# Hybrid trunk layer: order of the mixer's column pairs, four attention chains in step, and a fourth seven-product unit in the first branch gates

## Chip, cores and metric

The kernel runs on one core of one Trainium2 chip. The metric is the device time of one execution in microseconds, and the median of several runs is the kernel's time. Traces come from one further execution under the hardware profiler.

## The reference

One layer of a trunk on x (1, 256, 2048): a SwiGLU half-step, a mixer of two gated recurrences side by side, a second SwiGLU half-step, with an RMSNorm before and behind each. The change touches only the mixer:

```python
proj = u @ w_in
(g_q, g_k, g_v, g_out, g_code, h_q, h_f, h_i, h_out, z_gla, z_hgrn) = jnp.split(proj, offsets, axis=-1)
...
o_gla = merge_heads(rms_norm(o_gla, gla_norm)).astype(u.dtype) * jax.nn.silu(g_out)
...
log_f = jnp.logaddexp(jnp.log(lb), jnp.log1p(-lb) + jax.nn.log_sigmoid(h_f.astype(jnp.float32)))
h_k = -jnp.expm1(log_f)
o_hgrn = chunked_gated_linear_attention(
    split_heads(jax.nn.silu(h_q), HGRN_HEADS), split_heads(h_k, HGRN_HEADS),
    split_heads(h_i, HGRN_HEADS), split_heads(log_f, HGRN_HEADS))
...
merged = (jax.nn.sigmoid(z_gla + b_branch_gates[0]) * (o_gla @ w_branch_gla)
          + jax.nn.sigmoid(z_hgrn + b_branch_gates[1]) * (o_hgrn @ w_branch_hgrn))
return merged @ w_out
```

GLA has 4 heads (key width 128, value width 256), HGRN2 has 8 heads of 128. Both are causal recurrences with a decay for each key element.

## The kernel before

**Stages.** The layer runs as FFN1, mixer, FFN2. The 256 rows are two tiles of 128 (t = 0, 1). Weights come from HBM in float32, in chunks of two 128-row tiles by 512 columns. Each is split into a high part (`whi`, ScalarE's copy, L158) and a low part (`wlo`, VectorE's subtraction, L160). Every product is then three matmuls: high by high, high weight by low operand, low weight by high operand (L164, L165, L166). All operands are laid out beforehand, so TensorE waits for nothing but weights.

**Pairs.** The mixer's projections are computed in pairs of 512-wide column blocks (`gemm_pair`, called by `two`). The 2048 rows of the contraction make eight units of two row tiles. A plain unit is two chunks (one for each block), with 12 matmuls for each. Some units are seven-product units (`seven`): a Strassen-like scheme takes 7 products of three matmuls instead of 8, and pays with sums of weights (`wsum`, `raw`) that VectorE forms, ScalarE copies (`wsumh`) and VectorE splits (`wsuml`). The sums of the operand x for them are made once, by `operand_sums`. With the sums of three units (`SUMS`) a pair has three sevens; once a fourth unit's sums are there (`FOUR`), four. At the end of a pair `share` and `close` add the products that the sevens share (`psum`) to the accumulators c in PSUM. A ring of five buffers holds split weights, and three hold the rows of sums. `steps` is the order of chunks and sevens in a pair; with `late` the sevens stand at places 6, 8 and 10.

**Side work.** What isn't a projection is written as generators that `Side.pump` advances, once for each plain chunk and twice in a seven. Light ones are transposes, gates and dots: each yields and goes on one step at a pump. Heavy ones are the attention chains (`attention`), one for each row tile and branch group: seven levels (1, 2, 4, ... 64 wide), in each of which TensorE multiplies small blocks (L899, 32 matmuls in the trace for a narrow level), VectorE scales k and q (L915, L918), picks scores (`own`, L920) and multiplies decays into totals (`tot`, L939). `full` holds the heavy ones off around a seven; with `fast` they step at each pump where no light one is left, else at every second; at most two chains step in one pump. The instructions of all this stand in one order for each engine, which the program fixes when it is built: an engine issues strictly in that order, and a split behind a level waits for the level.

**The mixer's pairs** are, in order: GK/GV, GV+CB/GO, GO+CB/HF, HI/HO, HQ+CB/HF+CB, HI+CB/HO+CB, then the first two branch gates ZG (a pair), two branch blocks, and the other gates and blocks (G is GLA, H is HGRN; Q, K, V, O are queries, keys, values and output gates, F forget gates, I HGRN's values; +CB is the second block of 512 columns). The GLA chains (two row tiles) begin behind the first pair, the first HGRN chains behind the third, the second behind the fifth. The forget gates are computed by `hgrn_gates`: transposes, two sigmoids (L1068, L1069), and for each of four heads two affine copies with the lower bound, "borders" below (L1072, L1073).

## Time and profile before

| | |
|---|---|
| median of 3 runs | 2053.48 us (2053.33 to 2054.65) |
| the profiled execution | 2053.87 us |
| its span in the trace | 2052.0 us |
| granted TensorE clock, mean | 0.998 |
| HBM read and written | 406.11 MB, 4.19 MB |
| ScalarE | 1331.7 us busy, 65% |

A row of a timeline gives the start of an instruction (or of a run of like ones, "x2"), its length, engine and line, the tiles out<-in, and in brackets the idle time before it with what ended it. Instructions of one engine overlap at their ends, so that the distance from start to start is what an engine pays for one; where VectorE has an x2 row, the next row's start tells. PE is TensorE, DVE VectorE, ACT ScalarE.

### The profile page before, as it was taken

The page shows a single profiled execution, that of the slowest core. Times are in us where ns is not written, and L with a number is a line of the kernel's source. Part 1 is how long each engine was busy: PE and PEld are TensorE (multiplying, and loading weights), DVE is VectorE, ACT ScalarE, POOL GpSimd, SP SyncE. Part 2 cuts the span into 40 slices and gives each one's busy share as a digit, 9 for nine tenths or more (in the row PEclk, how much of TensorE's full clock was granted, in tenths as well). Part 3 has the DMA queues.
Part 4 walks back from the last instruction along what each step waited for, and adds up shares of the span by engine and source line. Part 5 has one row for each costly group of instructions (what it writes and reads, how often), then busy time and mean ns, then how long its engine had stood idle before and what let it go on. Part 6 is the DMA issues. An engine that isn't in the chain of part 4 may idle for free.

```text
span 2052.0 us, 29001 instructions
## 1 busy us (share of the span) xinstructions
PE 2039.7 (99%) x10287; PEld 1696.1 (83%) x10287; DVE 1896.4 (92%) x2237; ACT 1331.7 (65%) x1740; POOL 40.1 (2%) x87
## 2 busy tenths in 40 slices
PE   9999999999999999999999999999999999999998
PEld 8888888888888888878888888888888888888886
DVE  8999999999899889989999898889999999989997
ACT  7666666666666577577655565666666766676663
POOL 1000000000000100000000000010000000000000
PEclk9999999999999999999999999999999999999999
DMA  8777677776657567556566568757777777776664
GB/s 254 228 215 230 200 220 223 214 223 212 224 183 234 163 215 226 164 173 194 169 199 196 180 219 226 233 161 207 245 199 222 220 215 208 220 235 195 216 194 144
DMA packets 256282, 425.60 MB, mean 207 GB/s; under 512 B 72116, under 2 KB 80503, under 8 KB 256136
## 3 DMA queue, kind: packets, MB, share of 16 engines
q1 hardware_dynamic: 196624, 401.80, 62.0%
q10 hardware_dynamic: 59512, 21.94, 5.6%
q8 instruction: 80, 1.31, 0.3%
q14 instruction: 66, 0.54, 0.1%
HBM read 406.11 MB, written 4.19 MB: 200 GB/s over the span
## 4 chain that ended last, share of the span: by engine, by line
PE 92%; DVE 3%; ACT 2%; DMA 2%; issue 1%; POOL 0%; SPq 0%; DVEq 0%; POOLq 0%; ACTq 0%
PE c L164 22%; PE c L165 22%; PE c L166 22%; PE p L166 6%; PE p L164 6%; PE p L165 6%; PE mm L164 2%; PE mm L166 2%; PE mm L165 2%; DVE h L546 1%; PE ps L404 1%; DVE wlo L160 1%; DVE held L160 1%; DMA raw<-in_w_in_dram 1%; PE ps L899 0%
## 5 line engine op out<-in xcount | busy, mean ns | idle before, releaser
L158 ACT ACTIVATE whi<-raw 128x1024 fp32r<-128x1024 f32 (+3 forms) x486 | 491.6, 1025 | 176.7 <-PE c L165 75.7
L160 DVE TENSOR_TENSOR wlo<-raw,whi 128x1024 fp32r<-128x1024 f32 (+3 forms) x486 | 567.9, 1182 | 38.4 <-ACT whi L158 36.1
L164 PE MATMUL c<-whi,xhi 128*128 128x512 f32 (+1 forms) x1350 | 526.1, 390 | 0.7 <-DVE hq L842 0.5
L165 PE MATMUL c<-whi,xlo 128*128 128x512 f32 (+1 forms) x1350 | 522.7, 387 | 0.0
L166 PE MATMUL c<-wlo,xhi 128*128 128x512 f32 (+1 forms) x1350 | 522.2, 387 | 0.0
L250 DVE TENSOR_TENSOR wlo<-raw,whi 128x1024 fp32r<-128x1024 f32 x264 | 313.9, 1218 | 17.6 <-ACT whi L289 14.3
L164 PEld LDWEIGHTS c<-whi,xhi 128*128 128x128 f32 x1350 | 253.4, 188 | 52.2 <-issue 1.2
L166 PEld LDWEIGHTS c<-wlo,xhi 128*128 128x128 f32 x1350 | 253.4, 188 | 50.7 <-DVE wlo L160 0.2
L165 PEld LDWEIGHTS c<-whi,xlo 128*128 128x128 f32 x1350 | 253.5, 188 | 49.2
L289 ACT ACTIVATE whi<-raw 128x1024 fp32r<-128x1024 f32 x132 | 139.6, 1057 | 214.1 <-DVE raw L250 141.7
L250 DVE TENSOR_TENSOR wsuml<-wsum,wsumh 128x1536 fp32r<-128x1536 f32 x132 | 231.1, 1751 | 12.7 <-ACT wsumh L291 12.7
L164 PE MATMUL c<-whi,hkhi 128*128 128x512 f32 x534 | 207.7, 389 | 0.0
L165 PE MATMUL c<-whi,hklo 128*128 128x512 f32 x534 | 207.7, 389 | 0.0
L166 PE MATMUL c<-wlo,hkhi 128*128 128x512 f32 x534 | 207.7, 389 | 0.0
L287 ACT ACTIVATE wsumh<-wsum 128x1024 fp32r<-128x1024 f32 x132 | 138.8, 1051 | 87.4 <-DVE wsum L250 42.9
L285 ACT ACTIVATE whi<-raw 128x1024 fp32r<-128x1024 f32 x132 | 139.1, 1054 | 73.5 <-PE c L165 49.3
L250 DVE TENSOR_TENSOR wsum<-raw,raw 128x1024 f32<-128x1024 f32 x132 | 160.9, 1219 | 22.8 <-DMA raw<-in_ffn_w_down_dram 13.2
L165 PEld LDWEIGHTS c<-whi,hklo 128*128 128x128 f32 x534 | 100.2, 188 | 20.9
L164 PEld LDWEIGHTS c<-whi,hkhi 128*128 128x128 f32 x534 | 100.2, 188 | 20.9
L166 PEld LDWEIGHTS c<-wlo,hkhi 128*128 128x128 f32 x534 | 100.2, 188 | 20.7
L250 DVE TENSOR_TENSOR c<-c,psum 128x512 f32<-128x512 f32 x143 | 94.4, 690 | 8.7 <-PE c L166 8.4
L250 DVE TENSOR_TENSOR wsum<-raw 128x512 f32<-128x512 f32 x132 | 91.2, 691 | 3.8
(347 smaller groups left out, 3072.0 us busy)
## 6 DMA issues: line engine op xcount, KB each, us to landing
raw<-in_ffn_w_down_dram SPq DMA_DIRECT2D x120, 512.0 KB, 4.8
raw<-in_w_in_dram SPq DMA_DIRECT2D x104, 512.0 KB, 4.4
raw<-in_ffn_w_gate_dram SPq DMA_DIRECT2D x90, 512.0 KB, 4.6
raw<-in_ffn_w_up_dram SPq DMA_DIRECT2D x90, 512.0 KB, 3.9
raw<-in_ffn_w_gate_dram SPq DMA_DIRECT2D x140, 256.0 KB, 4.1
raw<-in_ffn_w_up_dram SPq DMA_DIRECT2D x140, 256.0 KB, 4.2
raw<-in_w_in_dram SPq DMA_DIRECT2D x128, 256.0 KB, 3.4
raw<-in_ffn_w_down_dram SPq DMA_DIRECT2D x104, 256.0 KB, 3.8
```

Of the source, the lines that this page charges most:

```text
L158: last[0] = nc.scalar.activation(hi, src, AF.Copy)
L160: nc.vector.tensor_tensor(lo, src, hi.bitcast(F32), op=ALU.subtract)
L164: nc.tensor.matmul(ps, lhsT=xhi, rhs=whi, start=start, stop=False)
L165: nc.tensor.matmul(ps, lhsT=xlo, rhs=whi, start=False, stop=False)
L166: nc.tensor.matmul(ps, lhsT=xhi, rhs=wlo, start=False, stop=stop)
L250: return nc.vector.tensor_tensor(o, x, y, op=op)
L285: nc.scalar.activation(ahi, ra, AF.Copy)
L287: nc.scalar.activation(hi[:, 0:2, :], wsum[:, 0:2, :], AF.Copy)
L289: nc.scalar.activation(bhi, rb, AF.Copy)
L404: end = nc.tensor.transpose(dst_ps[:, i * P:(i + 1) * P], src[:, i * P:(i + 1) * P], ident)
L546: nc.vector.scalar_tensor_tensor(h[t][n], acc[t][n], r1, h[t][n], op0=ALU.mult, op1=ALU.add)
```

## The change

It consists of these parts:

- The pairs' columns are regrouped: GK/HF, GV/GO, GV+CB/GO+CB, then HI/HO, HQ+CB/HF+CB and HI+CB/HO+CB as before. HF comes two pairs sooner, GV and GV+CB each a pair later. All pairs from the second on have their sevens late.
- The four first chains (GLA's two and the first HGRN two) wait for each other (`group`) and step together: while `side.wide` is set, up to four chains step at every second pump. It is set after GV/GO and cleared after the first branch gates.
- `attention` is divided: `begin` makes `own` and the first product as a light generator, `scores` copies the wide levels' scores behind the splits, `outputs` does the transposes and splits of a result later.
- `hgrn_gates` waits 3 or 4 pumps and spreads its borders over pumps, behind the splits; `own_keys` makes the key sigmoid and the dots, 8 or 10 pumps later.
- `operand_sums` for the fourth unit is spawned before the pair HI+CB/HO+CB instead of after the first branch gates, so that the first branch gates ZG have four sevens, at places 3, 5, 7 and 9.

In the new kernel the line numbers are 5 higher for the splits and matmuls (L163, L165, L169 to L171); a level's lines are L938, L954, L957, L959 and L975, the sigmoids and borders L1095, L1096, L1103 and L1104. In all, TensorE has three 128x512 matmuls fewer, VectorE four operations more (those of one seven less two plain splits), ScalarE two more; SP issues four loads of 256 KB in place of two of 512 KB.

```diff
-        self.fast = False
+        self.fast = self.wide = False
...
-        self.due = not self.light if self.fast else len(self.heavy) < 2 or not self.due
-        if self.due and not self.full:
+        if self.full:
+            return
+        if self.fast and not self.wide:
+            self.due = not self.light
+        else:
+            self.due = len(self.heavy) < 2 or not self.due
+        if self.due:
             steps = 0
             for g in list(self.heavy):
                 steps += self._step(self.heavy, g) != Side.WAITS
-                if steps == 2:
+                if steps == (4 if self.wide else 2):
                     break
...
-        if late:
+        if len(sevens) > len(SUMS):
+            at = range(3, 3 + 2 * len(sevens), 2)
+        elif late:
             at = range(6, 6 + 2 * len(sevens), 2)
-        elif len(sevens) > len(SUMS):
-            at = range(3, 3 + 2 * len(sevens), 2)
...
-            def attention(t, qT, kT, fT, d, vs, gates, dv, br, b0):
+            begun = {}
+            def begin(qT, kT, fT, d):
                 while not all(id(x) in laid for x in (qT, kT, fT, d)):
-                    yield Side.WAITS
-                own = mp.tile([P, 4 * 32], F32, tag="own", name=nm("own"), bufs=2)
+                    yield
+                own = mp.tile([P, 4 * 32], F32, tag="own", name=nm("own"), bufs=4)
                 for i in range(4):
                     nc.scalar.activation(own[:, i * 32:(i + 1) * 32], diag, AF.Copy,
                                          scale=d[:, i:i + 1])
                 nc.vector.tensor_tensor(qT, qT, fT, op=ALU.mult)
-                yield
+                begun[id(qT)] = own
+            def outputs(on, key):
+                for _ in range(4):
+                    yield
...
+            def scores(sc, ps, c, late):
+                if late:
+                    yield
+                with behind_splits():
+                    for r0 in range(0, P, 2 * c):
...
+            def attention(t, qT, kT, fT, group, vs, gates, dv, br, b0):
+                while not all(id(x) in begun for x in group):
+                    yield Side.WAITS
+                own, late = begun[id(qT)], br == "h" and not b0
...
-                        for r0 in range(0, P, 2 * c):
...
+                        side.spawn(scores(sc, ps, c, late))
...
+                    side.spawn(outputs(on, (br, t, b0 + b)))
...
             def hgrn_gates(y, t, g, fT, kT):
-                yield
+                for _ in range(3 + t):
+                    yield
...
-                nc.scalar.activation(fT, tp, AF.Sigmoid)
-                nc.scalar.activation(kT, tp, AF.Sigmoid, scale=-1.0)
+                with behind_splits():
+                    nc.scalar.activation(fT, tp, AF.Sigmoid)
+                    nc.scalar.activation(kT, tp, AF.Sigmoid, scale=-1.0)
                 for i in range(4):
+                    if i % 2 == 0:
+                        for _ in range(1 + t):
+                            yield
                     sl, hd = slice(i * P, (i + 1) * P), slice(4 * g + i, 4 * g + i + 1)
-                    nc.scalar.activation(kT[:, sl], kT[:, sl], AF.Copy, scale=lc[:, hd])
-                    nc.scalar.activation(fT[:, sl], fT[:, sl], AF.Identity, scale=lc[:, hd],
-                                         bias=lb[:, hd])
+                    with behind_splits():
+                        nc.scalar.activation(kT[:, sl], kT[:, sl], AF.Copy, scale=lc[:, hd])
+                        nc.scalar.activation(fT[:, sl], fT[:, sl], AF.Identity, scale=lc[:, hd],
+                                             bias=lb[:, hd])
                 mark(fT, kT)
...
-            def attend(qT, kT, fT, dd, dv, br, b0):
+            def attend(qT, kT, fT, dd, dv, br, b0, group):
...
-                    side.heavy.append(attention(t, qT[t], kT[t], fT[t], dd[t], vs, gates, dv, br, b0))
+                    side.spawn(begin(qT[t], kT[t], fT[t], dd[t]))
+                    side.heavy.append(attention(t, qT[t], kT[t], fT[t], group, vs, gates, dv, br, b0))
                 return vs, gates
...
-            k, v, ready = two(O_GK, O_GV, (), cols(O_GV + CB), cols(O_GO))
+            def own_keys(y, q, k, d, t, row):
+                for _ in range(8 + 2 * t):
+                    yield
+                with behind_splits():
+                    nc.scalar.activation(k, y, AF.Sigmoid, scale=-1.0)
+                yield
+                yield from dots(q, k, d, row)
+            def hgrn(g, qs, qT, f, group=None):
+                fT, kT = [blk("hfT") for _ in range(NT)], [blk("hkT") for _ in range(NT)]
+                ys = [scaled(f[t], rs[t], "y") for t in range(NT)]
+                dd = [mp.tile([P, 4], F32, name=f"hd{g}{t}") for t in range(NT)]
+                for t in range(NT):
+                    side.spawn(hgrn_gates(ys[t], t, g, fT[t], kT[t]))
+                    side.spawn(own_keys(ys[t], qs[t], blk("hk"), dd[t], t, lambda: lc_rows[g]))
+                return attend(qT, kT, fT, dd, P, "h", g, group or qT)
...
+            k, f, ready = two(O_GK, O_HF, (), cols(O_GV), cols(O_GO))
...
-            vs, gates = attend(qT, kT, fT, dd, 256, "g", 0)
+            vs, gates = attend(qT, kT, fT, dd, 256, "g", 0, qT + hqT)
+            hvs, hgates = hgrn(0, hqs, hqT, f, qT + hqT)
+            v, go, ready = two(O_GV, O_GO, ready, cols(O_GV + CB), cols(O_GO + CB), late=True)
+            side.wide = True
             vs.append([scaled(v[t], rs[t], "v") for t in range(NT)])
-            v, go, ready = two(O_GV + CB, O_GO, ready, cols(O_GO + CB), cols(O_HF))
+            gates.append([silu(go[t], rs[t], h[t][0]) for t in range(NT)])
+            v, go, ready = two(O_GV + CB, O_GO + CB, ready, cols(O_HI), cols(O_HO), late=True)
             vs.append([scaled(v[t], rs[t], "v") for t in range(NT)])
-            gates.append([silu(go[t], rs[t], h[t][len(gates)]) for t in range(NT)])
-            go, f, ready = two(O_GO + CB, O_HF, ready, cols(O_HI), cols(O_HO), late=True)
-            gates.append([silu(go[t], rs[t], h[t][len(gates)]) for t in range(NT)])
-            def hgrn(g, qs, qT, f):
...
-            vs, gates = hgrn(0, hqs, hqT, f)
+            gates.append([silu(go[t], rs[t], h[t][1]) for t in range(NT)])
             side.spawn(lc_row(1))
             v, go, ready = two(O_HI, O_HO, ready, cols(O_HQ + CB), cols(O_HF + CB), late=True)
-            vs.append(values(v, 0))
-            gates.append(gates_of(go, 0))
+            hvs.append(values(v, 0))
+            hgates.append(gates_of(go, 0))
             q, f, ready = two(O_HQ + CB, O_HF + CB, ready, cols(O_HI + CB), cols(O_HO + CB), late=True)
             hqs = [silu(q[t], rs[t], blk("hq")) for t in range(NT)]
             vs, gates = hgrn(1, hqs, spawn_T(hqs, "hqT"), f)
+            side.spawn(operand_sums(x, new_part, sums))
             v, go, ready = two(O_HI + CB, O_HO + CB, ready, cols(O_ZG), cols(O_ZG + CB), late=True)
             vs.append(values(v, 1))
             gates.append(gates_of(go, 1))
             done("g")
             szs, ready = two_gates(0, O_ZG, 0, ready, first_of(a["w_branch_gla"], 0), late=True)
-            side.spawn(operand_sums(x, new_part, sums))
+            side.wide = False
             for n in range(2):
                 ms.append(branch_gla(n, szs[n], ready))
                 ready = ()
```

The order in which the engines issue changes at three places. The first is ScalarE around the first seven of the second pair (GV+CB/GO before, GV/GO after). Before, it stands so from the seven's sums (`wsumh_7280`); `whi_7288` is the copy of its second weights, and 7327 and 7345 are plain chunks behind it:

```order
L287 ACTIVATE wsumh_7280<-wsum_7279 128x1024
L428 DMA_TRANSPOSE turned_7211<-halves_7209 128x8x128
L289 ACTIVATE whi_7288<-raw_7278 128x1024
L291 ACTIVATE wsumh_7280<-wsum_7279 128x512
L820 COPY kT_7173<-ps_7213 128x512
L820 COPY kT_7174<-ps_7219 128x512
L158 ACTIVATE whi_7327<-raw_7325 128x1024
L882 ACTIVATE own_7229<-diag,gd_7175 128x32 x4
L882 ACTIVATE own_7235<-diag,gd_7176 128x32 x4
L158 ACTIVATE whi_7345<-raw_7343 128x1024
```

After, from the own parts on:

```order
L884 ACTIVATE own_7237<-diag,gd_7175 128x32 x4
L884 ACTIVATE own_7243<-diag,gd_7176 128x32 x4
L1095 ACT_TABLE_LOAD
L1095 ACTIVATE hfT_7177<-ps_7267 128x512
L1096 ACTIVATE hkT_7179<-ps_7267 128x512
L1104 ACTIVATE hfT_7177<-hfT_7177,lb,lc 128x128
L1103 ACTIVATE hkT_7179<-hkT_7179,lc 128x128 x2
```

Seven rows further, which are borders and the second row tile's sigmoids, it goes on so; `whi_7358` is the copy of this seven's second weights:

```order
L1103 ACTIVATE hkT_7180<-hkT_7180,lc 128x128
L1104 ACTIVATE hfT_7178<-hfT_7178,lb,lc 128x128
L1103 ACTIVATE hkT_7180<-hkT_7180,lc 128x128
L1104 ACTIVATE hfT_7178<-hfT_7178,lb,lc 128x128
L294 ACTIVATE whi_7358<-raw_7348 128x1024
L1201 ACTIVATE hk_7187<-y_7181 128x512
```

The own parts are followed by the table load, four sigmoids and twelve borders, and the second copy of the seven, which stood ahead of the own parts, now stands behind all of them.

The second place is VectorE at the start of the third pair (GO+CB/HF before, GV+CB/GO+CB after). Before, between two plain splits, 7790 and 7850, stand two gate products (L842), a level of the two GLA chains and two totals; the splits 7532 to 7730 are done by then:

```order
L160 TENSOR_TENSOR wlo_7790<-raw_7787,whi_7789 128x1024
L842 SCALAR_TENSOR_TENSOR h_0_81<-c_1542_7182,r_6194,h_0_81 128x512
L842 SCALAR_TENSOR_TENSOR h_0_85<-c_1544_7184,r_6331,h_0_85 128x512
L915 TENSOR_TENSOR kT_7173<-kT_7173,fT_6401 128x256
L918 TENSOR_TENSOR qT_6399<-qT_6399,fT_6401 128x256
L920 COPY_PREDICATED own_7229<-masks,ps_7570 128x64
L915 TENSOR_TENSOR kT_7174<-kT_7174,fT_6402 128x256
L918 TENSOR_TENSOR qT_6400<-qT_6400,fT_6402 128x256
L920 COPY_PREDICATED own_7235<-masks,ps_7592 128x64
L939 TENSOR_TENSOR tot_7591<-tot_7591 128x32
L939 TENSOR_TENSOR tot_7569<-tot_7569 128x16
L160 TENSOR_TENSOR wlo_7850<-raw_7847,whi_7849 128x1024
```

After, a level is that of four chains (the GLA two with their totals 7627 and 7649, whose rows stand just ahead with the two gate products, and the HGRN two shown here), and the next level follows a single split:

```order
L954 TENSOR_TENSOR hkT_7179<-hkT_7179,hfT_7177 128x256
L957 TENSOR_TENSOR hqT_6740<-hqT_6740,hfT_7177 128x256
L959 COPY_PREDICATED own_7485<-masks,ps_7672 128x64
L975 TENSOR_TENSOR tot_7671<-hfT_7177 128x256
L954 TENSOR_TENSOR hkT_7180<-hkT_7180,hfT_7178 128x256
L957 TENSOR_TENSOR hqT_6741<-hqT_6741,hfT_7178 128x256
L959 COPY_PREDICATED own_7539<-masks,ps_7694 128x64
L975 TENSOR_TENSOR tot_7693<-hfT_7178 128x256
L165 TENSOR_TENSOR wlo_7730<-raw_7727,whi_7729 128x1024
L954 TENSOR_TENSOR kT_7173<-kT_7173,tot_7627 128x128x2
L957 TENSOR_TENSOR qT_6399<-qT_6399,tot_7627 128x128x2
L959 COPY_PREDICATED own_7237<-masks,ps_7745 128x32x2
```

The split 7730, the pair's third chunk, stands behind the first level of all four chains; only the pair's first two chunks are split ahead of it.

The third place is VectorE at the end of the first branch gates ZG. Before, the additions to c, the four gate products (L1013) and the first operand sums stand ahead of a split of the first branch block, 10164:

```order
L250 TENSOR_TENSOR c_1991_9620<-c_1991_9620,psum_10037 128x512
L250 TENSOR_TENSOR c_1993_9622<-c_1993_9622,psum_10037 128x512
L250 TENSOR_TENSOR c_1992_9621<-c_1992_9621,psum_10038 128x512
L1013 SCALAR_TENSOR_TENSOR h_0_85<-c_1993_9622,r_6331,h_0_81 128x512
L250 TENSOR_TENSOR c_1994_9623<-c_1994_9623,psum_10038 128x512
L1013 SCALAR_TENSOR_TENSOR h_0_81<-c_1991_9620,r_6194,h_0_81 128x512
L1013 SCALAR_TENSOR_TENSOR h_1_86<-c_1994_9623,r_6331,h_1_82 128x512
L230 TENSOR_TENSOR sums_10099<-xhi_1313_6060,xlo_1314_6061 128x256
L1013 SCALAR_TENSOR_TENSOR h_1_82<-c_1992_9621,r_6194,h_1_82 128x512
L230 TENSOR_TENSOR sums_10099<-xhi_1328_6155,xlo_1329_6156 128x256
L160 TENSOR_TENSOR wlo_10164<-raw_10161,whi_10163 128x1024
```

After, the operand sums are gone from here, and a level of the two second HGRN chains stands between the gate products (L1038) and the block's second split, 10238 (the first, 10164, stands ahead of the additions to c):

```order
L255 TENSOR_TENSOR c_2029_9798<-c_2029_9798,psum_10132 128x512
L1038 SCALAR_TENSOR_TENSOR h_0_85<-c_2028_9797,r_6331,h_0_81 128x512
L1038 SCALAR_TENSOR_TENSOR h_1_86<-c_2029_9798,r_6331,h_1_82 128x512
L1038 SCALAR_TENSOR_TENSOR h_0_81<-c_2026_9795,r_6194,h_0_81 128x512
L1038 SCALAR_TENSOR_TENSOR h_1_82<-c_2027_9796,r_6194,h_1_82 128x512
L954 TENSOR_TENSOR hkT_9186<-hkT_9186,tot_9811 128x128x2
L957 TENSOR_TENSOR hqT_9182<-hqT_9182,tot_9811 128x128x2
L959 COPY_PREDICATED own_9648<-masks,ps_10193 128x32x2
L954 TENSOR_TENSOR hkT_9187<-hkT_9187,tot_9833 128x128x2
L957 TENSOR_TENSOR hqT_9183<-hqT_9183,tot_9833 128x128x2
L959 COPY_PREDICATED own_9707<-masks,ps_10214 128x32x2
L165 TENSOR_TENSOR wlo_10238<-raw_10235,whi_10237 128x1024
```

The level's six rows now stand ahead of the block's splits 10238 and 10256.

More of the change, by code (lines that the diff above doesn't have):

```diff
@@ L884, in attention @@
                 nc.vector.tensor_tensor(qT, qT, fT, op=ALU.mult)
+                begun[id(qT)] = own
+            def outputs(on, key):
+                for _ in range(4):
+                    yield
+                tp = ps_tile()
+                transpose4(tp, on)
+                hi, lo = [tiles4(blk("oT", F32R)) for _ in range(2)]
+                parts = 2 if key[0] == "g" else 1
+                for k in range(parts):
+                    src, dst, rest = [x[:, k::parts, :] for x in (tiles4(tp), hi, lo)]
+                    w = norms[key[0]][:, k:k + 1]
+                    nc.scalar.activation(dst, src, AF.Copy, scale=w)
+                    nc.vector.scalar_tensor_tensor(rest, src, w, dst.bitcast(F32),
+                                                   op0=ALU.mult, op1=ALU.subtract)
+                oT[key] = hi, lo
+            def scores(sc, ps, c, late):
[3 more added lines that the diff above has]
+                    for r0 in range(0, P, 2 * c):
+                        nc.scalar.copy(
+                            tiles4(sc)[r0:r0 + c, :, r0 + c:r0 + 2 * c],
+                            ps[r0:r0 + c, :4 * c].rearrange("p (h c) -> p h c", c=c))
                 yield
+            def attention(t, qT, kT, fT, group, vs, gates, dv, br, b0):
+                while not all(id(x) in begun for x in group):
+                    yield Side.WAITS
+                own, late = begun[id(qT)], br == "h" and not b0
                 tot, totals, at = fT, blk("tot"), 0
@@ L982, in attention @@
                                                        gates[b][t][:, cs], op0=ALU.mult, op1=ALU.mult)
+                    side.spawn(outputs(on, (br, t, b0 + b)))
                     yield
-                    yield
-                    tp = ps_tile()
-                    transpose4(tp, on)
-                    hi, lo = [tiles4(blk("oT", F32R)) for _ in range(2)]
-                    for k in range(dv // P):
-                        src, dst, rest = [x[:, k::dv // P, :] for x in (tiles4(tp), hi, lo)]
-                        w = norms[br][:, k:k + 1]
-                        nc.scalar.activation(dst, src, AF.Copy, scale=w)
-                        nc.vector.scalar_tensor_tensor(rest, src, w, dst.bitcast(F32),
-                                                       op0=ALU.mult, op1=ALU.subtract)
-                    oT[br, t, b0 + b] = hi, lo
             def o_lhs(br):
@@ L1194, in gates_of @@
                         for t in range(NT)]
-            vs, gates = hgrn(0, hqs, hqT, f)
+            k, f, ready = two(O_GK, O_HF, (), cols(O_GV), cols(O_GO))
+            ks = [scaled(k[t], rs[t], "k") for t in range(NT)]
+            kT = spawn_T(ks, "kT")
+            dd = spawn_dots(qs, ks, "gd")
+            vs, gates = attend(qT, kT, fT, dd, 256, "g", 0, qT + hqT)
+            hvs, hgates = hgrn(0, hqs, hqT, f, qT + hqT)
+            v, go, ready = two(O_GV, O_GO, ready, cols(O_GV + CB), cols(O_GO + CB), late=True)
+            side.wide = True
+            vs.append([scaled(v[t], rs[t], "v") for t in range(NT)])
+            gates.append([silu(go[t], rs[t], h[t][0]) for t in range(NT)])
+            v, go, ready = two(O_GV + CB, O_GO + CB, ready, cols(O_HI), cols(O_HO), late=True)
+            vs.append([scaled(v[t], rs[t], "v") for t in range(NT)])
+            gates.append([silu(go[t], rs[t], h[t][1]) for t in range(NT)])
             side.spawn(lc_row(1))
             v, go, ready = two(O_HI, O_HO, ready, cols(O_HQ + CB), cols(O_HF + CB), late=True)
-            vs.append(values(v, 0))
-            gates.append(gates_of(go, 0))
+            hvs.append(values(v, 0))
+            hgates.append(gates_of(go, 0))
             q, f, ready = two(O_HQ + CB, O_HF + CB, ready, cols(O_HI + CB), cols(O_HO + CB), late=True)
```

13 lines of the change are left out of this document (removed).

## The prediction

> **What bounds the kernel now.** I read the page first, for who is busy, then the windows of the mixer, then the timelines of single engines there.
>
> ```profile
> span 2052.0 us, 29001 instructions
> PE 2039.7 (99%) x10287; PEld 1696.1 (83%) x10287; DVE 1896.4 (92%) x2237; ACT 1331.7 (65%) x1740; POOL 40.1 (2%) x87
> 819.00:863.00 44.00, 44.00 (x496) 35.42 (x495) 43.56 (x77) 23.28 (x26) 0.53 (x1) 1.00 0.56 168
> ```
>
> TensorE sets the end: it works in 2039.7 of 2052.0 us. So a change can win only by giving it less to do or by removing a wait of it, and can lose by making it wait. The second thing to see is in the window row (sum, PE, weight loads, DVE, ACT, POOL, clock): in the pair in which the GLA chains step, VectorE works 43.56 of 44 us too. It has no reserve there; it merely keeps ahead of TensorE. All of the change lies between about 765 and 1200 us, and the weight loads' time lies beside the matmuls.
>
> **Prices on TensorE.**
>
> ```profile
> 781.71 0.39 PE L166 MATMUL c<-wlo,xhi 128*128 128x512 f32 x1
> 781.95 1.03 PE L404 MATMUL ps<-ident,k 128*128 128x128 f32 x8
> 783.05 0.40 PE L165 MATMUL c<-whi,xlo 128*128 128x512 f32 x1
> 788.27 0.39 PE L164 MATMUL p<-whi,xhi 128*128 128x512 f32 x1
> 811.85 0.39 PE L166 MATMUL p<-wsuml,xs 128*128 128x512 f32 x1
> 821.37 0.39 PE L166 MATMUL c<-wlo,xhi 128*128 128x512 f32 x1
> 821.68 0.74 PE L899 MATMUL ps<-qT,kT 128*32 128x16 f32 x64
> 822.68 0.39 PE L165 MATMUL c<-whi,xlo 128*128 128x512 f32 x1
> 934.31 0.39 PE L166 MATMUL c<-wlo,xhi 128*128 128x512 f32 x1
> 934.62 0.45 PE L899 MATMUL ps<-hqT,hkT 128*32 128x16 f32 x32
> 935.33 0.39 PE L165 MATMUL c<-whi,xlo 128*128 128x512 f32 x1
> ```
>
> From 811.85 to 821.37 stand 42 matmuls: 0.2267 us each, start to start (the 0.39 overlaps). A group of small matmuls between them costs what it adds to that: 64 of a level (two chains) take 821.37 to 822.68, less two matmuls (0.45), 0.86; 32 (one chain) take 1.02 less 0.45, 0.57. So a group has a fixed 0.28 and 0.29 for each chain; four chains in one group cost 1.44. Eight transposes add 1.34 less 0.45, 0.89.
>
> **Prices on VectorE,** start to start.
>
> ```profile
> 822.80 1.40 DVE L842 SCALAR_TENSOR_TENSOR h<-c,r,h 128x512 f32<-128x512 f32 x2
> 824.12 0.41 DVE L915 TENSOR_TENSOR kT<-kT,fT 128x256 f32<-128x256 f32 x1
> 824.45 0.42 DVE L918 TENSOR_TENSOR qT<-qT,fT 128x256 f32<-128x256 f32 x1
> ...
> 825.72 0.27 DVE L939 TENSOR_TENSOR tot<-tot 128x32 f32<-128x32 f32 x2
> 825.91 1.21 DVE L160 TENSOR_TENSOR wlo<-raw,whi 128x1024 fp32r<-128x1024 f32 x1
> ...
> 893.03 1.22 DVE L160 TENSOR_TENSOR wlo<-raw,whi 128x1024 fp32r<-128x1024 f32 x1
> 894.17 1.22 DVE L250 TENSOR_TENSOR wsum<-raw,raw 128x1024 f32<-128x1024 f32 x1
> ...
> 900.69 1.22 DVE L160 TENSOR_TENSOR wlo<-raw,whi 128x1024 fp32r<-128x1024 f32 x1
> 1055.08 1.21 DVE L250 TENSOR_TENSOR psum<-psum,p 128x1024 f32<-128x1024 f32 x1
> 1056.21 1.29 DVE L250 TENSOR_TENSOR c<-c,psum 128x512 f32<-128x512 f32 x2
> 1057.48 0.70 DVE L250 TENSOR_TENSOR c<-c,psum 128x512 f32<-128x512 f32 x1
> ```
>
> A level of two chains takes 824.12 to 825.72, 0.80 a chain; a gate product (L842) 0.66; a product of two rows' totals 0.33 at 128x256 (824.45 less 824.12, the same size) and 0.10 at 128x32. A plain split takes 1.14 (893.03 to 894.17), the six operations of a seven-product unit 6.5 (894.17 to 900.69), a 1024-wide sum of psum 1.13 and an addition of 512 to c 0.63. TensorE spends 12 matmuls on a plain chunk, 2.72, and 21 on a seven, 4.76. So **a seven costs VectorE 1.7 us more than it gives TensorE to do, a plain chunk 1.6 less**. Plain chunks, ahead of the sevens, must build the lead that the sevens and the chains use up.
>
> **What the change saves.** (1) The fourth seven of the ZG pair: 21 matmuls instead of 24, -0.68. (2) The level groups: 24 before, 19 after with the same matmuls in all, five times 0.28 is 1.4; the transposes and other groups that come to stand alone give back 0.55 by the order, -0.85. (3) A wait of before:
>
> ```profile
> L164 PE MATMUL c<-whi,xhi 128*128 128x512 f32 (+1 forms) x1350 | 526.1, 390 | 0.7 <-DVE hq L842 0.5
> 892.35 0.39 PE L165 MATMUL p<-wsumh,xs 128*128 128x512 f32 x1
> 893.17 0.50 PE L166 MATMUL p<-wsuml,xs 128*128 128x512 f32 x1 [0.43 <-DVE wsuml L250]
> ```
>
> 0.82 between two matmuls, less 0.23, is 0.59; behind it VectorE needs 7.66 for a seven and a plain split (893.03 to 900.69), while 33 matmuls take 7.48, so with the next two sevens about 1.0. It stands in the pair HI/HO, which after loses its gates and borders: -1.0. The group of plain matmuls shows 0.7 of waits in the whole span, 0.5 of it for hq, ahead of the change. Sum -2.5; there is nothing else to win, so **this is also the ceiling**: 2051.4 for the profiled execution.
>
> **Term A, ScalarE in the pair GV/GO.** HF now comes with GK, so its gates fall into the first seven of the next pair. In the order, ScalarE issues 8 own, a table load, four sigmoids of 128x512 and twelve borders ahead of the copy that this seven's second weights need; before, that copy stood ahead of them and no gate was near.
>
> ```profile
> 788.51 1.60 ACT L882 ACTIVATE own<-diag,gd 128x32 f32<-128x32 f32 x7 [0.65 <-DVE gd L862]
> 818.89 1.06 ACT L158 ACTIVATE whi<-raw 128x1024 fp32r<-128x1024 f32 x1 [0.19 <-PE c L165]
> 819.97 1.28 ACT L841 ACT_TABLE_LOAD   x1
> 821.27 0.69 ACT L841 ACTIVATE h<-c,r 128x512 f32<-128x512 f32 x1
> 869.34 0.58 ACT L1068 ACTIVATE hfT<-ps 128x512 f32<-128x512 f32 x1
> 870.30 0.50 ACT L1073 ACTIVATE hfT<-hfT,lb,lc 128x128 f32<-128x128 f32 x1
> 870.68 0.70 ACT L1072 ACTIVATE hkT<-hkT,lc 128x128 f32<-128x128 f32 x2
> 871.27 0.50 ACT L1073 ACTIVATE hfT<-hfT,lb,lc 128x128 f32<-128x128 f32 x1
> ```
>
> Prices: own 0.22; table load 1.28; sigmoid 0.48 (two from 869.34 to 870.30); hfT border 0.38, hkT border 0.30 (two from 870.68 to 871.27); copy 1.06. The own waited for gd until 788.51; after, one operation fewer stands ahead of gd on VectorE, some 0.75 earlier, 787.75. Then 8 own to 789.55, the load to 790.8, sigmoids to 792.75, six borders of each kind (4.1) to 796.8, the copy to 797.9. TensorE began this seven at 788.27; from there to the copy's product stand 30 matmuls (6.8) and eight transposes (0.89): 796.0. So 1.9 late, and the lo part of the same weights, 1.14 behind the copy, is due two matmuls (0.45) behind it: 0.7 more. **A = +2.5**; 1 if the burst starts an own's wait earlier, 3.5 if the next copies, queued behind six further sigmoids and borders, slip too. VectorE queues its own later splits behind this lo, so nothing is made up.
>
> [...]
>
> **Term B, four chains at a time in the pair GV+CB/GO+CB.** The first level group stands ten matmuls into this pair, and a level's VectorE rows need its result, so VectorE can't begin them earlier, whatever its lead. From the first level row to the plain split behind the third seven, the order gives it: three sevens 19.5; seven plain splits 8.0; three levels of four chains, twelve times 0.80, 9.6; two gate products 1.3; 24 totals (four at 0.33, twenty at about 0.12, between 0.33 and 0.10) 3.7: 42.1. TensorE, from the end of the first chain's matmuls to where it uses that split: three chains left of the group 0.87, 154 matmuls 34.9, two groups 2.88: 38.65. **B = +3.4**, between 2.4 and 4.5 (some 42 operations, each good to 0.025). In before, two chains and half the totals stepped here and three plain chunks were split beforehand; after, only two chunks are split when the pair begins. The pairs HI/HO and HQ/HF have less VectorE work than before by the order: nothing.
>
> **Term C, four sevens in ZG.** The same argument, from the first level of the second HGRN chains (it stands where ZG begins) to the first split of the first branch block: four sevens 26.0; eight plain splits 9.1; two levels of two chains 3.2; two ho gate products 1.3; totals 1.9; the close of ZG, two psum sums of 512 (as c, 1.26), one of 1024 (1.13), four c additions 2.5, 4.9; four gate products of ZG 2.6: 49.0. TensorE: the second chain 0.29, 188 matmuls 42.6, two groups 1.72: 44.6. The difference is 4.4; gate products may slip behind the need of TensorE's hi products, which the order puts first there, so I take **C = +4.1**, between 1.8 (the lead before the level group counts after all, and one split of slack at each end) and 4.8. The former three sevens at the pair's end left VectorE one seven less and a plain chunk more on TensorE's side: 1.7+1.6, which is why this place had no wait. The operand sums that now run a pair sooner lie in a pair where TensorE has 5 us more to do than VectorE by the order: nothing there, and no loss if that cover shrinks by 3.
>
> DMA: two loads of 512 KB become four of 256 KB in SP's queue, the same bytes, far ahead of their use: nothing.
>
> **Sum.** -2.5 + 2.5 + 3.4 + 4.1 = +7.5 on 2053.87: 2061.4. The median of the three runs, 2053.48, is 0.4 lower: **2061**. A difference under about 0.2%, 4.1 us, can hardly be measured on this kernel.
>
> **Rivals.**
> - **Slower than TensorE's saving, but covered in part.** One or two of the three terms fall away because a lead that I count as zero is there: 2053.5 - 2.5 + 2.5 to 6, 2053.5 to 2057. For it: VectorE's lead in plain stretches is several splits. Against it: the level groups and closes tie it to TensorE's place at each pair's start. Chance 0.22.
> - **The other side: all of it is covered.** The waits of VectorE for the level groups vanish if the lead carries over the pair's start; it decides at a lead of 3.4 us behind the first level of B and 4.4 at C. Then only the saving is left: 2053.48 less 2.5, 2051.0, not slower. Against it stands the order, in which levels precede the splits. Chance 0.10; a gain over 0.2% would need more than the ceiling, 0.03 of it.
> - [...] Chance 0.07.
> - **The change does not do what it says:** by the order it does; three matmuls fewer, one seven more, groups of 128 level matmuls. Chance 0.01.
>
> **How the numbers follow.** Forecast 0.60, taken as 2058 to 2064.5 (the bounds of A, B and C don't all fall the same way). With the rivals: slower by over 0.2% (above 2057.6) 0.68, the forecast, the drain and the edge of the partial cover; within 0.2% 0.29; faster 0.03. The range takes in the partial cover and the forecast, and leaves full cover out: 2053 to 2065.
>
> **What would show it.** A: TensorE waits for a whi, released by ScalarE, in the first seven of GV/GO, and VectorE for ScalarE beside it. B: TensorE waits for wlo and wsuml from the plain chunks to the last seven of GV+CB/GO+CB, with VectorE busy without a gap; groups of 128 level matmuls cost 1.44. C: the same from ZG's sevens into the first branch chunk. The wait at 893 is gone. Wrong would be: TensorE's waits in these three stretches under 3 us together, or a long wait elsewhere, as in the pair HI/HO.

## The result, and the profile after

| | before | after |
|---|---|---|
| median | 2053.53 us (6 runs, 2053.33 to 2054.65) | 2065.07 us (6 runs, 2063.27 to 2067.93) |
| ratio, 95% interval | | 1.0055 (1.0042 to 1.0068) |
| profiled execution | 2053.87 us | 2065.09 us |

The change makes the kernel 11.5 us slower. The forecast was 2061, and the time lies 4 us above it, at the very end of the range (2053 to 2065). The page of the new kernel, its span and busy times:

```profile
span 2063.3 us, 28989 instructions
PE 2042.7 (99%) x10284; PEld 1696.7 (82%) x10284; DVE 1901.9 (92%) x2241; ACT 1332.8 (65%) x1742; POOL 39.6 (2%) x87
```

The three matmuls fewer are there. TensorE's busy time is 3.0 us longer with less to do: a 512-wide matmul's row is 0.39 long where the next one usually starts after 0.227, so some 0.16 of each wait counts as busy, and so does the time lost to a slower clock (2.00 of 2.00 us busy at a granted 0.54 from 800 us, below). So the loss is read from its waits. The first six lines of the view of waits for TensorE, after (what waited, what it waited for, total, times, longest):

```profile
engine line waited for: us in total, times, longest us
PE c L169 <- ACT whi L294: 3.1, 3, 1.5
PE c L171 <- DVE wlo L165: 1.9, 3, 0.7
PE ps L938 <- DVE hqT L957: 1.8, 2, 1.4
PE ps L1369 <- POOL idle L1364: 1.3, 1, 1.3
PE p L169 <- DVE oT L901: 0.7, 1, 0.7
PE c L171 <- DVE wlo L255: 0.5, 1, 0.5
```

The 1.3 of POOL stands in the kernel before too. The first three lines and the last are made up of waits of the prediction's three terms. To size them by place I take each distance between two 512-wide matmuls in the mixer, less 0.227 and less the price of the small matmuls between them, and add up what exceeds 0.15. That gives 2.3 us before and 15.2 after:

| place | predicted | after |
|---|---|---|
| GV/GO, first seven (A): waits | 2.5 | 2.3 (1.63, 0.69) |
| the eight matmuls behind: slow clock | none | 1.6 |
| GV+CB/GO+CB (B) | 3.4 | 2.7 (0.40, 0.66, 0.90, 0.77) |
| HI/HO and the start of HQ+CB/HF+CB | nothing, the old wait of 1.0 goes | 1.8 (0.56, 0.79, 0.23, 0.23) |
| HI+CB/HO+CB | nothing | 1.8 (0.83 the largest) |
| ZG and first branch block (C) | 4.1 | 4.05 (0.79, 1.22, 2.04) |
| behind it | nothing | 0.9 |

The difference of 12.9, less 0.7 for the three matmuls, leaves some 1.0 for the groups if it is to be the 11.2 between the two profiled executions; the 1.0 is this remainder, not a measurement. In the fourth row only the 0.79 is a wait in the trace, at 925 us, five us into the pair HQ+CB/HF+CB, while HI/HO's gates are still being made; the other three stand beside level groups that come in pieces and are in part their price.

**A.** ScalarE's timeline after, the burst ahead of the first seven's second copy, and TensorE's behind it:

```profile
786.72 1.81 ACT L884 ACTIVATE own<-diag,gd 128x32 f32<-128x32 f32 x8
788.54 1.28 ACT L1095 ACT_TABLE_LOAD   x1
789.84 0.60 ACT L1095 ACTIVATE hfT<-ps 128x512 f32<-128x512 f32 x1
...
795.45 0.49 ACT L1104 ACTIVATE hfT<-hfT,lb,lc 128x128 f32<-128x128 f32 x1
795.83 1.06 ACT L294 ACTIVATE whi<-raw 128x1024 fp32r<-128x1024 f32 x1
```

```profile
795.09 0.39 PE L171 MATMUL c<-wlo,xs 128*128 128x512 f32 x1
796.94 0.50 PE L169 MATMUL c<-whi,xhi 128*128 128x512 f32 x1 [1.47 <-ACT whi L294]
797.28 0.40 PE L170 MATMUL c<-whi,xlo 128*128 128x512 f32 x1
798.20 0.63 PE L171 MATMUL c<-wlo,xhi 128*128 128x512 f32 x1 [0.52 <-DVE wlo L255]
798.62 0.63 PE L169 MATMUL p<-whi,xs 128*128 128x512 f32 x1
...
801.61 0.50 PE L170 MATMUL p<-wsumh,xs 128*128 128x512 f32 x1
```

The queue ran as worked out: own to 788.5, load, four sigmoids, twelve borders, copy; every step 1 us sooner than forecast, and TensorE came 0.7 sooner too. The table load is 1.28 long, and the first sigmoid starts 1.30 after its start, so 0.02 is paid beyond the load. Not foreseen is the spacing behind: from 798.20 on a matmul takes 0.43 instead of 0.227. The windows (length, PE, weight loads, DVE, ACT, POOL, granted clock, share and GB/s of DMA):

```profile
798.00:800.00 2.00, 1.80 (x5) 1.42 (x6) 1.93 (x4) 2.00 (x5) 0.00 (x0) 0.61 0.38 77
800.00:802.00 2.00, 2.00 (x7) 1.59 (x6) 2.00 (x3) 1.60 (x2) 0.00 (x0) 0.54 0.53 188
802.00:804.00 2.00, 2.00 (x11) 1.64 (x9) 1.60 (x2) 1.16 (x2) 0.00 (x0) 1.00 0.81 248
```

The granted clock is 0.61, then 0.54, and 1.00 again behind.

**B.** VectorE and TensorE at the start of GV+CB/GO+CB, after:

```profile
826.60 0.43 DVE L954 TENSOR_TENSOR kT<-kT,fT 128x256 f32<-128x256 f32 x1 [0.70 <-PE ps L938]
...
832.13 0.42 DVE L975 TENSOR_TENSOR tot<-hfT 128x256 f32<-128x256 f32 x1
832.47 1.23 DVE L165 TENSOR_TENSOR wlo<-raw,whi 128x1024 fp32r<-128x1024 f32 x1
833.60 0.43 DVE L954 TENSOR_TENSOR kT<-kT,tot 128x256 f32<-128x256 f32 x1
...
843.63 1.24 DVE L165 TENSOR_TENSOR wlo<-raw,whi 128x1024 fp32r<-128x1024 f32 x1
844.76 1.24 DVE L255 TENSOR_TENSOR wsum<-raw,raw 128x1024 f32<-128x1024 f32 x1
```

```profile
843.79 0.39 PE L170 MATMUL p<-whi,xlo 128*128 128x512 f32 x1
844.92 0.50 PE L171 MATMUL c<-wlo,xhi 128*128 128x512 f32 x1 [0.74 <-DVE wlo L165]
847.10 0.39 PE L170 MATMUL c<-whi,xs 128*128 128x512 f32 x1
848.10 0.50 PE L169 MATMUL c<-whi,xhi 128*128 128x512 f32 x1 [0.61 <-ACT whi L294]
```

VectorE waits 0.70 for the level group, as foretold, and then works without a gap: four splits in 18 us. The second wait shown names ScalarE's copy, but ScalarE had stood idle for 14.39 us until VectorE's sum `wsum` (844.76) was done; it copies that first, and then the weights, so this is VectorE's lateness too. Behind 848, which is in the pair's first seven, no wait of TensorE is left in this pair.

**C.** VectorE and TensorE in the first branch block:

```profile
1071.94 2.73 DVE L1038 SCALAR_TENSOR_TENSOR h<-c,r,h 128x512 f32<-128x512 f32 x4
1074.58 0.42 DVE L954 TENSOR_TENSOR hkT<-hkT,tot 128x256 f32<-128x256 f32 x1
1074.91 0.43 DVE L957 TENSOR_TENSOR hqT<-hqT,tot 128x256 f32<-128x256 f32 x1
```

```profile
1073.55 0.40 PE L170 MATMUL mm<-whi,oT 128*128 128x512 f32 x1
1075.39 0.45 PE L938 MATMUL ps<-hqT,hkT 128*32 128x16 f32 x32 [1.45 <-DVE hqT L957]
1076.19 0.45 PE L938 MATMUL ps<-hqT,hkT 128*32 128x16 f32 x32 [0.36 <-DVE hqT L957]
```

VectorE came late out of ZG, did four gate products, and only then the level that the next group of small matmuls needs. So the last and largest wait of C is one of a group, not of a split; the other two stand at ZG's first chunks and first seven.

### The profile page after: what moved, and what is told of

Same layout as the page of the kernel before. It is cut to its first block, busy times and chain, and to the rows that moved or that the text cites. A ratio compares the mean times of both kernels' runs of the same rounds, so it can differ in the third digit from the quotient of the medians.

```text
span 2063.3 us, 28989 instructions
## 1 busy us (share of the span) xinstructions
PE 2042.7 (99%) x10284; PEld 1696.7 (82%) x10284; DVE 1901.9 (92%) x2241; ACT 1332.8 (65%) x1742; POOL 39.6 (2%) x87
## 4 chain that ended last, share of the span: by engine, by line
PE 87%; DVE 7%; ACT 2%; issue 2%; DMA 1%; POOL 0%; DVEq 0%; POOLq 0%; ACTq 0%
PE c L169 21%; PE c L171 21%; PE c L170 21%; PE p L169 6%; PE p L171 6%; PE p L170 5%; PE mm L171 2%; PE mm L169 2%; PE mm L170 2%; DVE wlo L165 1%; DVE h L551 1%; DMA raw<-in_w_in_dram 1%; DVE wsum L255 1%; DMA raw<-in_ffn_w_down_dram 0%; PE ps L409 0%
## 5 line engine op out<-in xcount | busy, mean ns | idle before, releaser
L165 DVE TENSOR_TENSOR wlo<-raw,whi 128x1024 fp32r<-128x1024 f32 (+3 forms) x484 | 566.9, 1186 | 39.3 <-ACT whi L163 36.0
L163 ACT ACTIVATE whi<-raw 128x1024 fp32r<-128x1024 f32 (+3 forms) x484 | 489.0, 1024 | 173.2 <-PE c L170 69.9
L169 PE MATMUL c<-whi,xhi 128*128 128x512 f32 (+1 forms) x1343 | 522.6, 389 | 4.0 <-ACT whi L294 3.1
L171 PE MATMUL c<-wlo,xhi 128*128 128x512 f32 (+1 forms) x1343 | 516.6, 387 | 2.5 <-DVE wlo L165 1.9
L169 PEld LDWEIGHTS c<-whi,xhi 128*128 128x128 f32 x1343 | 252.1, 188 | 56.1 <-ACT whi L294 4.7
L171 PEld LDWEIGHTS c<-wlo,xhi 128*128 128x128 f32 x1343 | 252.1, 188 | 54.2 <-DVE wlo L165 2.9
L169 PE MATMUL c<-whi,hkhi 128*128 128x512 f32 x534 | 207.7, 389 | 0.0
L171 PE MATMUL c<-wlo,hkhi 128*128 128x512 f32 x534 | 207.7, 389 | 0.0
L171 PEld LDWEIGHTS c<-wlo,hkhi 128*128 128x128 f32 x534 | 100.2, 188 | 20.8
L169 PEld LDWEIGHTS c<-whi,hkhi 128*128 128x128 f32 x534 | 100.2, 188 | 20.8
```

The lines of the kernel that those rows point to most:

```text
L163: last[0] = nc.scalar.activation(hi, src, AF.Copy)
L165: nc.vector.tensor_tensor(lo, src, hi.bitcast(F32), op=ALU.subtract)
L169: nc.tensor.matmul(ps, lhsT=xhi, rhs=whi, start=start, stop=False)
L171: nc.tensor.matmul(ps, lhsT=xhi, rhs=wlo, start=False, stop=stop)
```

## The experiments

Each kernel was timed beside the kernel before on the same chip (e1 to e4 on one chip, e5 to e10 on another), 5 runs each unless noted; the medians of the kernel before there were 2053.2 to 2053.6. The runs of one kernel lie 1.9 to 4.4 us apart, so differences of 1 to 2 us between two rows are read from the traces, not from the medians.

| kernel | median us | ratio (interval) |
|---|---|---|
| e1_no_four | 2060.46 | 1.0036 (1.0023 to 1.0048) |
| e2_levels_out | 2060.65 | 1.0037 (1.0025 to 1.0050) |
| e3_gates_later | 2064.87 | 1.0059 (1.0045 to 1.0073) |
| e4_four_only | 2067.88 | 1.0072 (1.0060 to 1.0085) |
| e5_two_sevens | 2064.20 | 1.0050 (1.0037 to 1.0063) |
| e6_both | 2065.28 | 1.0055 (1.0042 to 1.0068) |
| e7_all_three (11 runs) | 2057.77 | 1.0021 (1.0012 to 1.0030) |
| e8_same_again (the new kernel) | 2064.53 | 1.0059 (1.0045 to 1.0073) |
| e9_borders_out | 2063.20 | 1.0048 (1.0034 to 1.0062) |
| e10_early_three | 2061.51 | 1.0040 (1.0026 to 1.0054) |

**e1_no_four: is C the fourth seven?**

```diff
-            side.spawn(operand_sums(x, new_part, sums))
             v, go, ready = two(O_HI + CB, O_HO + CB, ...
...
             side.wide = False
+            side.spawn(operand_sums(x, new_part, sums))
```

> The new kernel, but the fourth unit's operand sums are made after the first branch gates again, so these have three sevens. Theory (the four sevens of ZG cost VectorE more than TensorE gives it time for): the waits of 0.79 and 1.22 us after ZG's first group and the 2.0 us in the first branch block go, about 4.0 us, and three matmuls come back, 0.7: 3.3 us under the new kernel, about 2061.7. Rival (the waits come from the second chains' levels and the outputs that stand there, whatever the sevens): they stay, and the time is 0.7 us over the new kernel.

Measured 2060.46, 4 us or more under the new kernel on either measurement (2065.07, 2064.53). All three waits of C are gone from the trace, the 0.83 in HI+CB/HO+CB too; 0.63 at 1015 us and 0.72 in the branch block are new. C comes with the fourth seven, and having it costs far more than the 0.7 that it saves. The edit takes three things away together: the seven, its operand sums a pair earlier, and the early places 3 to 9 (the three sevens stand at 6, 8 and 10). No run separates them. The traces bound the part of the sums: VectorE begins ZG's first level 0.4 us behind the end of that level's group in the new kernel (1029.12 against 1028.71) and 1.5 behind it in e1 (1028.48 against 1027.03), but in e1 one more split and both gate products are done by then, 1.14 and 1.3 us. So VectorE enters ZG some 1.4 us less far with the sums; the rest of the 4 us arises in ZG itself.

**e2_levels_out: is B VectorE's work on the chains?**

```diff
+                    cut = late and lv < 3
-                    if not last or t == 0:
+                    if (not last or t == 0) and not cut:
...
-                    if c < 32:
+                    if cut:
+                        pass
+                    elif c < 32:
```

> The new kernel without VectorE's scaling of k and q and its picking of scores in the first three levels of the two first HGRN chains (left out, so their output differs); the totals and TensorE's groups stay. That takes six times 0.80, 4.8 us, from VectorE in the pair GV+CB/GO+CB. Theory (VectorE's work on four chains makes TensorE wait there): the waits of 0.39, 0.66, 0.90 and 0.77 us of that pair go, 2.7 us, others stay: about 2062.4. Rival (the groups' own time or ScalarE bounds that pair): no change beyond 0.5 us.

Measured 2060.65, about 4 under the new kernel, more than expected. The trace has no wait over 0.15 us between 800 and 873 us, and the 0.79 at 925 us, behind HI/HO, is gone with B. So B is VectorE's work on the levels, and what is lost around HI/HO is its remainder.

**e3_gates_later: is A the burst?**

```diff
-                for _ in range(3 + t):
+                for _ in range(3 + t if g else 5 + t):
```

> The new kernel with the first forget gates begun two pumps later, so that ScalarE's table load, sigmoids and borders stand behind both copies of the first seven of GV/GO. Theory (this burst ahead of the copy is all of term A): the waits of 1.47 and 0.52 us at 795 to 798 us and the eight slow matmuls behind them go, 4.0 us: about 2061. Rival (the burst only moves the wait: the next seven's sums and copies then stand behind it): 2 us or more of wait appears at the second seven, and the time stays within 1.5 us of the new kernel.

Measured 2064.87: nothing gained. The waits at 795 and 797 us are gone. But 0.45 and 0.22 stand at the pair's third seven, and the next pair's waits grew from 2.7 to 3.9 us; its level groups now stand apart, GLA's first and HGRN's four matmuls later. Two groups more cost their fixed part as well (0.28 us each in the kernel before), and in this execution the slow clock came behind C (granted 0.76 from 1074 to 1076 us, 0.50 from 1076 to 1078). The rival is right in its result, though not quite by its mechanism.

**e4_four_only: is the regrouping needed for C?** On the kernel before:

```diff
+            side.spawn(operand_sums(x, new_part, sums))
             v, go, ready = two(O_HI + CB, O_HO + CB, ...
...
             szs, ready = two_gates(0, O_ZG, 0, ready, ...
-            side.spawn(operand_sums(x, new_part, sums))
...
-        if late:
+        if len(sevens) > len(SUMS):
+            at = range(3, 3 + 2 * len(sevens), 2)
+        elif late:
             at = range(6, 6 + 2 * len(sevens), 2)
-        elif len(sevens) > len(SUMS):
-            at = range(3, 3 + 2 * len(sevens), 2)
```

> The kernel before with only the fourth operand sums a pair sooner and so four sevens in the first branch gates; no regrouped pairs, no chains in step. Theory (four sevens with the chains' levels in that stretch run VectorE out of lead): three matmuls less, and 2 to 4 us of waits at the end of ZG and in the first branch block: 2055 to 2057. Rival (the chains of the new kernel are needed for it): no wait there, 2052.8.

Measured 2067.88, slower than the whole change; neither theory gave that. C's mechanism is there, with 1.70 us at the first branch block, but the rest is another: the second chains' last level group stands at 1237 us, against 1150 in the kernel before, and their results come late. By the code four sevens hold the chains back (`full`). The view of TensorE's waits of this kernel, and its timeline where the last results come:

```profile
PE ps L404 <- DVE on L981: 4.5, 4, 1.5
PE ps L404 <- DVE hkT L915: 2.7, 1, 2.7
```

```profile
1249.11 1.10 PE L404 MATMUL ps<-ident,on 128*128 128x128 f32 x4 [1.21 <-DVE on L981]
1250.88 0.33 PE L404 MATMUL ps<-ident,on 128*128 128x128 f32 x1 [0.67 <-DVE on L981]
```

At 1242 us, ahead of the last branch blocks, TensorE does the second chains' products one after another and waits for their norms, where there are no projections left to hide them. Against the kernel before it loses 13 us there alone; some 3 of them the kernel before had spent on the same products at 1199 us. So the regrouping does buy something: with the chains earlier, a fourth seven no longer delays their end into this place (last level group at 1142 us in the new kernel).

**e5_two_sevens: do the sevens of that pair make B?**

```diff
-            v, go, ready = two(O_GV + CB, O_GO + CB, ready, cols(O_HI), cols(O_HO), late=True)
+            v, go, ready = two(O_GV + CB, O_GO + CB, ready, cols(O_HI), cols(O_HO), late=True,
+                                sevens=SUMS[:2])
...
```

> The new kernel with two sevens instead of three in GV+CB/GO+CB: TensorE gets three matmuls more, 0.7 us, VectorE 6.5 less two plain splits, 4.2 us, less. Theory (VectorE's work in that pair is term B): the waits of 2.7 us there go, and the 0.8 us at 924 us with them, as with the levels left out: 2.5 to 3 us under the new kernel, about 2062.3. Rival (one row of sevens less saves nothing once the chains stand there): waits stay, 0.7 us over the new kernel.

Measured 2064.20. All four waits of B stand as before (0.39, 0.69, 0.90, 0.77); only those around HI/HO went. My theory fell: B is over by the first seven. A seven with a plain chunk takes VectorE 7.66 against TensorE's 7.48, so three of them add only 0.5 us. The levels among the plain chunks ahead of them are it.

**e6_both: with e5 and e3 together**

> As e5_two_sevens, and the first forget gates begun two pumps later as in e3_gates_later. Theory (the later gates saved nothing in e3 because the next pair's VectorE deficit took up what A had cost, and the groups stood apart): with that deficit gone too, A's 2.3 us are gained in full, less 0.8 for three groups more and 0.5 at the second seven: 1 to 2 us under e5, about 2061. Rival (A never cost anything beyond what some later wait takes): same as e5 within 0.5 us.

Measured 2065.28, no better than e5. A's waits are gone again and B's are 3.9. The rival is the nearer: later gates only move the cost.

**e7_all_three: e6 with three sevens in ZG**

> As e6_both, and three sevens in the first branch gates as in e1_no_four. Theory (three separate terms that add up): another 4 to 5 us less than e6, about 2056; what is left over the kernel before is 0.7 for the seven given up, some waits of 0.3 to 0.8 behind the chains and the outputs. Rival (another term that no wait shows): above 2058.

Measured 2057.77, between theory and rival, the best variant, and still slower than before (1.0021, 1.0012 to 1.0030). It is 7.5 us under e6, more than the 4 to 5 of the theory; the profiled execution of e6 has a mean granted clock of 0.998, that of e7 0.999. B is most of what remains: 0.20, 0.85, 0.97, 0.90 and 0.76 us. No version here beats the kernel before.

**e8_same_again: the same kernel, profiled again**

> The new kernel unchanged, for a second profile and for its time on the same chip as these. If the run of matmuls at twice the distance (eight of 0.43 us behind the wait at 797 us) belongs to the kernel, it is there again at the same place; if it depends on the moment, it is elsewhere or missing, while the waits at 795, 837, 844, 847, 1033, 1036 and 1074 us are there within 0.1 us.

The waits are there again within 0.1 us, but at A they are 1.90 and 0.69, and behind them the matmuls keep their distance; the first four rows of that stretch:

```profile
796.64 0.50 PE L169 MATMUL c<-whi,xhi 128*128 128x512 f32 x1 [1.74 <-ACT whi L294]
796.98 0.39 PE L170 MATMUL c<-whi,xlo 128*128 128x512 f32 x1
797.90 0.50 PE L171 MATMUL c<-wlo,xhi 128*128 128x512 f32 x1 [0.53 <-DVE wlo L255]
798.24 0.40 PE L169 MATMUL p<-whi,xs 128*128 128x512 f32 x1
```

The granted clock is 1.00 from 794 to 802 us here, where the first profile has 0.54 from 800 us: the slow clock belongs to the execution, not to the kernel.

**e9_borders_out: A without moving anything else**

```diff
+                    if g == 0:
+                        continue
                     sl, hd = slice(i * P, (i + 1) * P), slice(4 * g + i, 4 * g + i + 1)
```

> The new kernel without the first forget gates' borders (the affine copies with the lower bound are left out for the first HGRN group, so its output differs). The copy of the first seven of GV/GO then stands behind the own parts, the table load and two sigmoids alone, 5 us sooner, and the first level group stays whole. Theory (A is ScalarE's burst, and the later terms count from their own groups, so that terms add): the waits at 795 and 797 us, 2.3 to 2.6 us, go, and the pair after keeps its 2.7: 2062.5. Rival (what A cost was only ahead of the wait at the next pair's start, as e3 suggests): the waits in the next pair grow by 1 us or more, and the time stays within 1 us of the new kernel's.

Measured 2063.20, 1.3 to 1.9 us under the new kernel. The intervals overlap, so the traces must carry the reading. A's waits went, B stayed (0.48, 0.51, 0.73, 0.79), but 0.49 and 0.50 came at the pair's third seven, where TensorE waits for VectorE's splits. So A is worth about 1.5 us net of the slow clock, between theory and rival: the delay at A covered a shortfall of VectorE's.

**e10_early_three: sevens early in GV/GO, no fourth in ZG**

```diff
-            v, go, ready = two(O_GV, O_GO, ready, cols(O_GV + CB), cols(O_GO + CB), late=True)
+            v, go, ready = two(O_GV, O_GO, ready, cols(O_GV + CB), cols(O_GO + CB))
...
-                for _ in range(3 + t):
+                for _ in range(3 + t if g else 4 + t):
...
```

> As e1_no_four, and the pair GV/GO with its sevens early again (places 4, 7 and 10 as in the kernel before) and the first forget gates one pump later, so that ScalarE's burst stands behind the copies of the first seven, with the level groups as in the new kernel. Theory: e1's 2060.5 less the 2.4 of A, 2058. Rival (A is taken up by the next pair): 2060 to 2060.5. If the chains' stepping alone were at fault (and not that pair's missing lead), the waits at the level groups stay at 2.7 us although sevens no longer stand at the end of GV/GO.

Measured 2061.51, no better than e1 (the intervals overlap). The copies of the first seven stand ahead of the burst now, but TensorE waits 2.9 us inside that seven, at 793.8 us, until the second sigmoid has read the transposes in PSUM. By the code the seven's product p takes its PSUM tile from the same ring as those transposes, so the burst probably holds TensorE by a tile instead of a copy; no run shows the tile itself. B stays at 2.8 (0.17, 0.97, 0.89, 0.77). The condition set beforehand is not met by the edit: the third seven stands at place 10, two chunks ahead of the pair's end, in both orders, and only the first two stand earlier. So e10 says that B does not hang on the place of these two; that the chains' stepping makes B is shown by e2.

## Why the prediction was right and where it was short

- **TensorE sets the end, and VectorE has no reserve: right.** All losses but the slow clock are read at TensorE, and e1, e2 and e9 take waits away by taking work from VectorE or ScalarE.
- **The saving of 2.5: 1.5 to 1.7 of it came.** The three matmuls are gone, and the groups, taken as the remainder of the account, saved about what was worked out, though the trace has 20 level groups and not 19. "A wait of before ... -1.0" is the step that failed: the old wait at 893 us is gone, but HI/HO and the start of the next pair have 1.8 us of new losses. e2 and e5 remove most of them by lightening the pair ahead; VectorE enters HI/HO without a lead. The claim that this pair has less work was not the point.
- **Term A, +2.5: mechanism and wait right (2.3, in the second profile 2.6),** with the queue as listed. Short by 1.6 us of slow clock in the profiled execution. "Nothing is made up" was wrong: without A (e9) about 1 us of waits comes at the third seven, so A had covered them.
- **Term B, +3.4: mechanism right, 2.7, place half right.** VectorE does wait for the level group, and the deficit starts there (e2). But I let it grow to the third seven; it is complete at the first (e5), and the sum hid that sevens and plain chunks nearly balance.
- **Term C, +4.1: 4.05,** and e1 takes it away with the fourth seven. I expected waits for splits; half of it is a level group that waits for VectorE. The sum says "the first split of the first branch block", but it counts the close and the gate products and so runs to the second, as the order has it. That 4.1 and 4.05 agree so closely is luck: the bounds were 1.8 to 4.8.
- **The operand sums "nothing there": nearly.** VectorE stood 2.71 us for ScalarE's part of them (row below), and 0.83 us of TensorE's waits follow at 1001 us; without them (e1) that wait is gone, and 0.63 stands at 1015 instead.

```profile
989.12 0.69 DVE L165 TENSOR_TENSOR xs<-sums,xs 128x512 fp32r<-128x512 f32 x1 [2.71 <-ACT xs L163]
```

- **The rivals.** Covering leads did not exist: none of the three terms fell away. The drain that the chances count is shown by no run: a table load is 1.28 long and ScalarE's next instruction starts 1.30 behind its start, before (819.97 to 821.27) and after (788.54 to 789.84). The sum came out 4 us short because losses that I set to nothing add 3 to 4 us, less what the kernel before had of them (around HI/HO, HI+CB/HO+CB, the branch blocks), and the slow clock 1.6, less 0.7 at B.

The runs of the new kernel scatter over 4.7 us, those of before over 1.3 to 2.4. The granted clock of each run points to episodes of slow clock: over both measurements of the new kernel, the three runs with a mean of 0.999 took 2063.3 to 2063.8 us, those with 0.998 2064.4 to 2065.2 and once 2068.2, the two with 0.997 2066.9 and 2067.9. One episode takes 1.7 us of clock (half of the 3.41 us at 798 us in the profiled execution), 0.0008 of the span. So the kernel without an episode takes about 2063.4, and the median has about one. That is a reading of rounded means; the one run at 2068.2 does not fit it.

What stays open: how C divides among the number of sevens in ZG, their early places and the sums ahead of them, and how much of the 1.8 around HI/HO is a wait.

## What to carry over

When two engines are both near 100% in a stretch, sum each one's work between two points where one must wait for the other (here from the level group to the next seven), not over a whole stage. Moving side work so that it falls together saves its fixed cost (0.28 us a group here) but puts all its load on one stretch, and the engine that was just keeping ahead falls behind. And an optimisation that trades one engine's time for another's, like a seven for two plain chunks (0.7 us of TensorE for 4.2 of VectorE), pays only where the second has that time.

## What the runs showed of the hardware

Behind some waits of TensorE the granted clock falls to half. In the new kernel it is 0.50 from 798.42 to 801.84 us, for 3.41 us: eight matmuls of 0.43 us instead of 0.227, 1.6 us lost beside the wait. The windows of four profiles, with TensorE's busy time in each window:

| profile | windows, us | TensorE busy, us | granted clock |
|---|---|---|---|
| the new kernel, A | 798:800, 800:802, 802:804 | 1.80, 2.00, 2.00 | 0.61, 0.54, 1.00 |
| e10, the wait of 2.8 | 791:793, 793:795, 795:797, 797:799 | 0.02, 1.21, 2.00, 2.00 | 1.00, 0.70, 0.50, 0.95 |
| e3, C | 1072:1074, 1074:1076, 1076:1078, 1078:1080 | 0.57, 1.65, 2.00, 2.00 | 1.00, 0.76, 0.50, 0.89 |
| e5, C | 1071:1073, 1073:1075, 1075:1077, 1077:1079 | 0.57, 1.64, 2.00, 2.00 | 1.00, 0.71, 0.50, 0.93 |

The same waits stand in other executions without it. At A, e8 has idle times of 1.74 and 0.53 us, against 1.47 and 0.52 in the first profile of the same kernel, and its granted clock is 1.00 in every window from 794 to 802. At C, TensorE's two waits for hqT come to 1.8 us, the longer 1.4, in the new kernel, in e3 and in e5 alike; the granted clock from 1060 to 1080 us is 1.00 in the new kernel. So in these traces the length of a wait alone does not tell whether the clock falls behind it. What does is not shown.
